# A two-layer hybrid transformer on one core: the projection gets weight memory of its own, and the attention's PSUM is split two ways for its high output and three for scores

## The chip, the cores and the metric

One core of one Trainium2 chip runs the whole program. The metric is device time in microseconds (us). TensorE multiplies, VectorE (DVE), ScalarE (ACT) and GpSimd (POOL) do the elementwise work, and SyncE (SP) issues most DMAs. "Half clock" below means TensorE's granted clock of 1.2 GHz instead of 2.4.

## The reference, cut to what matters

All arithmetic is float32, over 2048 tokens of width 1024 and a context prefix of 256 tokens.

```python
# layer 0: 8 latent heads (keys of 64+32) and 8 grouped-query heads (2 key heads of 64)
h = modulate(x, shift, scale) @ w_in                  # and the same for the context
o_a = softmax(q_a k_a^T * A_SCALE) v_a                # 2048 queries, 256 + 2048 keys, 16 heads
o_b = softmax(q_b k_b^T * B_SCALE) v_b
y = concat([o_a * silu(g_a), o_b * silu(g_b)]) @ w_out
x = layer_norm(ALPHA * x + gate * y)
# layer 1: gated MLP that mixes tokens in chunks of 128
u, v, g = split(modulate(x, shift, scale) @ w_in)
v = layer_norm(gelu(v)); mixed = w_s @ v + b_s
y = (gelu(u) * mixed * silu(g)) @ w_out
out = layer_norm(ALPHA * x + gate * y)
```

## The kernel before

Each float32 operand of a large product is split into a high part (rounded to TensorE's fp32r format) and a low part (the rest), and a product is the sum of two or three fp32r matmuls. `split` makes the two parts: on ScalarE and VectorE, or, with `pool`, both on GpSimd.

There are three phases. **phase1** (0 to about 690 us) projects the inputs and writes keys, queries, values and gates to DRAM. **attention** (about 690 to 2357 us) works through 64 items, one per head and block of 512 queries (`work`, head by head): items 0 to 31 are latent heads, 32 to 63 grouped-query heads. An item has 18 steps, one for each 128 keys. For a step, `score` makes three (latent) or two (grouped-query) matmuls into a PSUM tile `s`, ScalarE takes the exponential twice (`ph` rounded to high, then in place in `s`), and `low` subtracts on VectorE: `pl = s - ph`, which frees `s`. In one or two steps of an item GpSimd makes both parts instead, from a copy `pf`. `mul` multiplies the values with `ph` into PSUM tile `oh` and with `pl` into `ol`. `add` sums `ph` on GpSimd for the softmax's denominator, and `total` splits that sum (`sh`, `sl`) for two more matmuls in the last `mul` of the item. `take` copies `ol` to `ob` on ScalarE, `finish` adds `oh` to it on VectorE (two instructions), multiplies by the gate (`gt`) and stores it. For a later item, 18 `peak` matmuls into PSUM tile `m` and 18 maxima on VectorE (`mx`) find the largest score of each query row. The last of them gives `nm`, which goes to DRAM (`NM`) and comes back as a row of the queries (`q<-NM`, `row`). The first scores of that item need that row.

The eight PSUM banks are: four for `s`, two for `m`, one each for `oh` and `ol`. The order of the work is written out by hand: `at(time, unit)` gives each unit a time in steps, the units are sorted by it, and `InOrder` keeps the instructions of one engine in that order. In step s there are: `score` at s, `mul` at `place` + 0.3, `peak` at s + 0.6, the maximum 0.7 later, `low` at s + 1.6. `place` lies 4 steps behind the score, plus `LATE[t]` for the first steps of an item, since `oh` and `ol` must be read first. For the last four items (the same head) there are no `add`s, and the gate is multiplied on VectorE. While they run, `z_load` and `z_split` prepare the first 512 tokens of the projection's input on GpSimd. `recip` inverts the denominators by way of DRAM.

**phase3** (about 2357 us to the end) takes four blocks of 512 tokens: the projection by `e_w_out` (`token_major`, PSUM `acc`) with norm, transposes (`tp`), then the second layer. `weights` loads 512 KB and splits it. Its first calls are gathered in `pre`, split on GpSimd. Instructions not bound by `InOrder` are placed by the compiler where their operands and memory are ready. Memory is laid out in the order of the pools and of the first use of a tag, and a tile waits for whatever tile lay in its place. In phase3 the pool `p3`, which holds the weight tiles `w`, `wh`, `wl`, the residual `t` and `gate_e`, lies in place of the attention's tiles, and the pool `p3c` of constants above it, in memory that the attention doesn't use.

Of the kernel before, what the change touches and what calls it, by code (L numbers as in the profile page):

```python
# [19 lines left out]
P = 128  # L20
D = 1024
# [36 lines left out]
def split(e, h, l, src, pool=False):  # L58

    if pool:  # L60
        e.nc.gpsimd.tensor_scalar(out=h, in0=src, scalar1=1.0, scalar2=0.0, op0=ALU.mult, op1=ALU.add)
        e.nc.gpsimd.tensor_tensor(out=l, in0=src, in1=h.bitcast(F32), op=ALU.subtract)  # L62
    else:
        e.nc.scalar.activation(h, src, AF.Copy)  # L64
        e.nc.vector.tensor_tensor(out=l, in0=src, in1=h.bitcast(F32), op=ALU.subtract)  # L65
# [462 lines left out]
def z_split(e, hl, z, pool=False):  # L528
    nc = e.nc
    h, l = hl  # L530
    (nc.gpsimd if pool else nc.vector).tensor_tensor(out=z, in0=l.bitcast(F32), in1=h.bitcast(F32), op=ALU.mult)
    split(e, h, l, z, pool)
# [111 lines left out]
def attention(e):  # L644
# [6 lines left out]

    LATE = (3.0, 2.6, 2.2, 1.8, 1.4, 1.0, .6, .3)
    with tc.tile_pool(name="atc", bufs=1, reuse_waits="tile") as cp, \
# [36 lines left out]
        def score(s):  # L690
# [4 lines left out]
            ks = slice(t * P, (t + 1) * P)  # L695
            ps = pp.tile([P, CH], F32, name="s", tag="s", bufs=4)
            m = NOPE + ROPE
# [43 lines left out]
        def mul(s):  # L741
# [3 lines left out]
            if t == 0:  # L745
                gates[i] = sp.tile([P, CH], F32, name="gt", tag="gt", bufs=2)
                nc.sync.dma_start(gates[i][:DV], e.G[h * DV:(h + 1) * DV, g * CH:(g + 1) * CH])
                acc[i] = [pp.tile([P, CH], F32, name="o" + q, tag="o" + q, bufs=1) for q in "hl"]
            ph, pl, _ = pts.pop(s)
# [16 lines left out]
        def finish(i):  # L766
            h, g = work[i]
            cs = slice(g * CH, (g + 1) * CH)
            ob, (oh, ol) = outs.pop(i), acc.pop(i)
            DVE.tensor_tensor(out=ob[:DV], in0=oh[:DV], in1=ob[:DV], op=ALU.add)  # L770
            DVE.tensor_tensor(out=ob[:DV], in0=oh[DV:], in1=ob[:DV], op=ALU.add)
            (DVE if i >= NW - NG else POOL).tensor_tensor(out=ob[:DV], in0=ob[:DV], in1=gates.pop(i)[:DV], op=ALU.mult)
            nc.sync.dma_start(e.SU[h:h + 1, cs], ob[DV:DV + 1])
            (nc.scalar if i == NW - 1 else nc.sync).dma_start(e.O[h * DV:(h + 1) * DV, cs], ob[:DV])

        def recip(b):

            view = lambda t: t[:, b * CH:(b + 1) * CH].rearrange("h (p j) -> h p j", p=8)
            rs = sp.tile([P, CH // 8], F32, name="rs", tag="rs", bufs=2)
            nc.sync.dma_start(rs, view(e.SU))  # L780
            nc.vector.reciprocal(rs, rs)
            nc.sync.dma_start(view(e.R1), rs)

# [16 lines left out]
        for s in range(NW * NTT):  # L800
# [8 lines left out]
            place = s + (LAGP if t in parts else LAG + (LATE[t] if t < len(LATE) else 0))  # L809
            at(place + 0.3, mul, s)  # L810
            if t == NTT - 1:
# [17 lines left out]
        for k in range(NK):  # L829
            at(end - (NG - 1) * NTT + 4 * k + 17, lambda k: z_split(e, e.Z[0][k], sp.tile([P, CH], F32, name="zt", tag="zt", bufs=2), True), k)  # L830
        for _, _, (f, *args) in sorted(units):
# [3 lines left out]
def phase3(e):  # L835
    nc, tc, I = e.nc, e.tc, e.ins
    NB = SEQ // CH
    with tc.tile_pool(name="p3", bufs=2, reuse_waits="tile") as sp, \
            tc.tile_pool(name="p3c", bufs=1, reuse_waits="tile") as cp, \
            tc.tile_pool(name="p3ps", bufs=1, space=PSUM, reuse_waits="tile") as pp:  # L840
# [26 lines left out]
        def late_constants():  # L867
# [4 lines left out]
            C["wsl"] = cp.tile([P, 8, P], F32R, name="wsl")  # L872
            w = sp.tile([P, 8, P], F32, name="w", tag="w", bufs=2)
            nc.sync.dma_start(w, I["wsT"])
# [4 lines left out]
        def wtile(q):  # L879
            return sp.tile([P, 1024], F32R if q else F32, name="w" + q, tag="w" + q, bufs=3 if q else 2)  # L880

# [65 lines left out]
        def even_out(b, Z, X, T, halfway=None, stagger=False, pre=()):  # L947
# [14 lines left out]
            token_major(Z, I["e_w_out"], 0, evac, halfway, b == 0, pre)  # L962
            if b == 0:
                constants()
            for k in range(NK):
# [7 lines left out]
        def odd_in(b, X, Z, T, v):  # L973
# [28 lines left out]
            for j in range(16):  # L1002
# [20 lines left out]
                if b + 1 < NB:  # L1023
                    if 2 <= j < 10:
                        z_split(e, Z[j - 2], tmp("y", 3))
                    if j < len(Z.groups):
                        z_load(e, b + 1, Z.groups[j], nc.gpsimd)
                if 4 <= j < 8:
                    nc.gpsimd.tensor_tensor(out=T[:, j - 4, :], in0=T[:, j - 4, :], in1=C["eg"], op=ALU.mult)
                    nc.gpsimd.tensor_tensor(out=T[:, j - 4, :], in0=T[:, j - 4, :], in1=C["eb"], op=ALU.add)  # L1030
            gated(7, st)
# [6 lines left out]
        def odd_out(b, Z, T):  # L1038
            xr = [T[:, t, :] for t in range(4)]

            def evac(t, cc, ps):
# [9 lines left out]


        w, h = ([wtile(q) for i in range(2)] for q in ("", "h"))
        ge, T = (sp.tile(x, F32, name=n, bufs=1) for n, x in (("gate_e", [P, D]), ("t", [P, 4, D])))
        l = [wtile("l") for i in range(2)]
        pre = [weights(I["e_w_out"].rearrange("(k p) f -> p k f", p=P)[:, 2 * kk:2 * kk + 2, :CH], 2, (h[kk], l[kk]), w[kk], True)
               for kk in range(2)]
        C["gate_e"] = ge
        nc.sync.dma_start(ge, e.M[0].partition_broadcast(P))
        residual(0, T, nc.sync)  # L1060
        V = sp.tile([P, 4, D], F32, name="v", bufs=1)
        A, B = e.Z[0], ring(e, True)
# [131 lines left out]
```

## Time and profile before

| | |
|---|---|
| median of 3 runs | 3374.85 us (3371.83 to 3386.05) |
| profiled execution, time and span | 3379.72 us, 3377.9 us |
| TensorE busy | 3209.4 us, 95% of the span, 13,698 matmuls |
| VectorE, ScalarE, GpSimd busy | 2555.7, 1890.6, 1763.6 us |

The profile is of one execution. Busy time counts an engine's own instructions, and a TensorE that is busy all the time can still run at half clock. Times in rows are microseconds from the start of the span. Engines: PE is TensorE's matmuls, SPq the queue of SyncE.

### The profile page before, as it was taken

The page shows a single profiled execution, that of the slowest core. Times are in us where ns is not written, and L with a number is a line of the kernel's source. Part 1 is how long each engine was busy: PE and PEld are TensorE (multiplying, and loading weights), DVE is VectorE, ACT ScalarE, POOL GpSimd, SP SyncE. Part 2 cuts the span into 40 slices and gives each one's busy share as a digit, 9 for nine tenths or more (in the row PEclk, how much of TensorE's full clock was granted, in tenths as well). Part 3 has the DMA queues.
Part 4 walks back from the last instruction along what each step waited for, and adds up shares of the span by engine and source line. Part 5 has one row for each costly group of instructions (what it writes and reads, how often), then busy time and mean ns, then how long its engine had stood idle before and what let it go on. Part 6 is the DMA issues. An engine that isn't in the chain of part 4 may idle for free.

```text
span 3377.9 us, 40485 instructions
## 1 busy us (share of the span) xinstructions
PE 3209.4 (95%) x13698; PEld 2435.5 (72%) x13698; DVE 2555.7 (76%) x3626; ACT 1890.6 (56%) x3259; POOL 1763.6 (52%) x1413
## 2 busy tenths in 40 slices
PE   7999999989999999999999999997899999999998
PEld 3886777767777777776666666665678778778786
DVE  4847894688888888888988989897655765855846
ACT  3433342267777777777777777775243353353342
POOL 3312431279999999998888888842302301301201
PEclk9999999999999999999999999998899999999999
DMA  6456655642212322122101111112533433433332
GB/s 229 141 166 203 205 165 166 176 89 59 60 37 50 63 59 59 35 54 62 28 25 27 36 40 27 29 29 38 167 100 106 132 117 107 140 107 108 106 94 75
DMA packets 187185, 314.09 MB, mean 93 GB/s; under 512 B 53264, under 2 KB 79184, under 8 KB 185056
## 3 DMA queue, kind: packets, MB, share of 16 engines
q1 hardware_dynamic: 179088, 284.08, 30.0%
q0 software_dynamic: 7808, 27.28, 2.6%
q8 instruction: 108, 1.77, 0.3%
q14 instruction: 101, 0.83, 0.2%
q10 hardware_dynamic: 80, 0.13, 0.0%
HBM read 240.71 MB, written 70.73 MB: 92 GB/s over the span
## 4 chain that ended last, share of the span: by engine, by line
PE 68%; DVE 7%; DMA 5%; issue 4%; ACT 2%; POOL 1%; SPq 0%; POOLq 0%; ACTq 0%; DVEq 0%
PE s L587 17%; PE ol L587 10%; PE oh L587 7%; PE m L587 7%; PE acc L910 4%; PE acc L911 3%; PE acc L1008 3%; PE acc L1007 3%; PE acc L1009 3%; PE acc L912 3%; DMA NM<-nm 3%; DVE mx L587 2%; PE ps L175 1%; PE ps L176 1%; PE ps L177 1%
## 5 line engine op out<-in xcount | busy, mean ns | idle before, releaser
L587 POOL TENSOR_TENSOR sa<-sa,ph 128x512 f32<-128x512 f32 x728 | 939.1, 1290 | 70.7 <-ACT ph L587 24.9
L587 DVE TENSOR_REDUCE mx<-m 128x1 f32<-128x512 f32 x1124 | 768.7, 686 | 154.3 <-PE m L587 128.6
L587 PE MATMUL s<-q,k 96*128 96x512 f32 (+2 forms) x2880 | 867.9, 399 | 12.0 <-DMA q<-NM 11.5
L587 ACT ACTIVATE ph<-s 128x512 fp32r<-128x512 f32 x1064 | 634.1, 596 | 337.8 <-PE s L587 320.0
L587 DVE TENSOR_TENSOR pl<-s,ph 128x512 fp32r<-128x512 f32 x1064 | 726.0, 683 | 41.6 <-ACT s L587 39.8
L587 PEld LDWEIGHTS s<-q,k 96*128 96x128 f32 (+2 forms) x2880 | 543.2, 190 | 151.6 <-issue 10.6
L587 ACT ACTIVATE s<-s 128x512 f32<-128x512 f32 x1064 | 633.4, 595 | 0.0
L587 PE MATMUL m<-k,q 128*128 128x512 f32 (+1 forms) x1250 | 457.6, 383 | 34.2 <-DVE mx L587 30.9
L587 PE MATMUL oh<-ph,v 128*128 128x512 f32 x1152 | 461.1, 400 | 14.3 <-DVE ob L587 13.5
L587 PE MATMUL ol<-pl,v 128*65 128x512 f32 x1152 | 455.5, 395 | 0.0
L64 ACT ACTIVATE wh<-w 128x1024 fp32r<-128x1024 f32 x154 | 163.2, 1059 | 492.2 <-PE acc L912 233.1
L65 DVE TENSOR_TENSOR wl<-w,wh 128x1024 fp32r<-128x1024 f32 x154 | 220.0, 1429 | 276.5 <-ACT wh L64 276.2
L587 PEld LDWEIGHTS m<-k,q 128*128 128x128 f32 (+1 forms) x1250 | 228.8, 189 | 173.0 <-DVE mx L587 88.9
L1018 POOL TENSOR_TENSOR u<-u,y 128x512 f32<-128x512 f32 x32 | 63.5, 1984 | 417.7 <-ACT y L1017 417.7
L587 PEld LDWEIGHTS oh<-ph,v 128*128 128x128 f32 x1152 | 218.3, 190 | 85.0 <-PE s L587 24.2
L176 PE MATMUL ps<-xl,wh 128*128 128x512 f32 (+1 forms) x640 | 251.3, 393 | 7.5 <-DVE xl L167 7.5
L175 PE MATMUL ps<-xh,wh 128*128 128x512 f32 (+1 forms) x640 | 250.6, 392 | 6.6 <-POOL wh L146 4.0
L177 PE MATMUL ps<-xh,wl 128*128 128x512 f32 (+1 forms) x640 | 249.8, 390 | 1.6 <-DVE wl L147 1.6
L587 PEld LDWEIGHTS ol<-pl,v 128*65 128x65 f32 x1152 | 158.7, 138 | 49.1
L910 PE MATMUL acc<-wh,k 128*128 128x512 f32 x384 | 158.6, 414 | 34.4 <-DVE y L1044 18.8
L911 PE MATMUL acc<-wl,k 128*128 128x512 f32 x384 | 157.5, 410 | 1.2 <-POOL wl L62 1.2
L146 POOL TENSOR_SCALAR wh<-wr 128x1024 fp32r<-128x1024 f32 (+1 forms) x48 | 57.9, 1207 | 189.9 <-PE ps L176 119.3
(300 smaller groups left out, 5458.8 us busy)
## 6 DMA issues: line engine op xcount, KB each, us to landing
w<-in_wug SPq DMA_DIRECT2D x64, 512.0 KB
wr<-in_w SPq DMA_DIRECT2D x38, 512.0 KB
w<-in_e_w_out SPq DMA_DIRECT2D x32, 512.0 KB
w<-in_o_w_in SPq DMA_DIRECT2D x32, 512.0 KB
w<-in_o_w_out SPq DMA_DIRECT2D x32, 512.0 KB
wr<-in_e_w_mod SPq DMA_DIRECT2D x24, 512.0 KB
wr<-in_o_w_mod SPq DMA_DIRECT2D x24, 512.0 KB
q<-QB SPq DMA_DIRECT2D x96, 128.0 KB
```

Of the source, the lines that this page charges most:

```text
L64: e.nc.scalar.activation(h, src, AF.Copy)
L65: e.nc.vector.tensor_tensor(out=l, in0=src, in1=h.bitcast(F32), op=ALU.subtract)
L175: nc.tensor.matmul(out, lhsT=wh(k), rhs=xh(k), start=i == 0, stop=False)
L176: nc.tensor.matmul(out, lhsT=wh(k), rhs=xl(k), start=False, stop=False)
L177: nc.tensor.matmul(out, lhsT=wl(k), rhs=xh(k), start=False, stop=i == n - 1)
L587: i = getattr(self.engine, name)(*args, **kw)
L910: nc.tensor.matmul(ps[t], lhsT=h[:, ts], rhs=w[0][:, k, :], start=first, stop=False)
L911: nc.tensor.matmul(ps[t], lhsT=h[:, ts], rhs=w[1][:, k, :], start=False, stop=False)
L912: nc.tensor.matmul(ps[t], lhsT=l[:, ts], rhs=w[0][:, k, :], start=False, stop=last)
L1007: nc.tensor.matmul(ps, lhsT=w[0][:, k, :], rhs=h, start=k == 0, stop=False)
L1008: nc.tensor.matmul(ps, lhsT=w[0][:, k, :], rhs=l, start=False, stop=False)
L1009: nc.tensor.matmul(ps, lhsT=w[1][:, k, :], rhs=h, start=False, stop=k == NK - 1)
```

## The change

It has these parts. In the attention: `oh` gets two PSUM banks and `s` three. `LATE` is shortened to four smaller delays. `mul` is placed 0.4 of a step later, which puts it behind `peak` in each step. The gate is always multiplied on GpSimd, and `z_split` there joins the written order. For the last four items the output goes by GpSimd's queue, and for the last the other small DMAs by ScalarE's. In phase3: the pools are laid out in another order (constants lowest, then the working tiles, then a new pool `p3w` for weight tiles, `gate_e` and the residual), three weight tiles are made ahead instead of two, `constants()` is called before the projection, and the four tiles of the residual are scaled and shifted in eight calls spread over eight passes instead of four.

```diff
 def split(e, h, l, src, pool=False):
     if pool:
-        e.nc.gpsimd.tensor_scalar(out=h, in0=src, scalar1=1.0, scalar2=0.0, op0=ALU.mult, op1=ALU.add)
-        e.nc.gpsimd.tensor_tensor(out=l, in0=src, in1=h.bitcast(F32), op=ALU.subtract)
+        pool = e.nc.gpsimd if pool is True else pool
+        pool.tensor_scalar(out=h, in0=src, scalar1=1.0, scalar2=0.0, op0=ALU.mult, op1=ALU.add)
+        pool.tensor_tensor(out=l, in0=src, in1=h.bitcast(F32), op=ALU.subtract)
...
 def z_split(e, hl, z, pool=False):
-    (nc.gpsimd if pool else nc.vector).tensor_tensor(out=z, in0=l.bitcast(F32), in1=h.bitcast(F32), op=ALU.mult)
+    (pool or nc.vector).tensor_tensor(out=z, in0=l.bitcast(F32), in1=h.bitcast(F32), op=ALU.mult)
...
-    LATE = (3.0, 2.6, 2.2, 1.8, 1.4, 1.0, .6, .3)
+    LATE = (1.2, .9, .6, .3)
...
-            ps = pp.tile([P, CH], F32, name="s", tag="s", bufs=4)
+            ps = pp.tile([P, CH], F32, name="s", tag="s", bufs=3)
...
-                acc[i] = [pp.tile([P, CH], F32, name="o" + q, tag="o" + q, bufs=1) for q in "hl"]
+                acc[i] = [pp.tile([P, CH], F32, name="o" + q, tag="o" + q, bufs=1 + (q == "h")) for q in "hl"]
...
-            (DVE if i >= NW - NG else POOL).tensor_tensor(out=ob[:DV], in0=ob[:DV], in1=gates.pop(i)[:DV], op=ALU.mult)
-            nc.sync.dma_start(e.SU[h:h + 1, cs], ob[DV:DV + 1])
-            (nc.scalar if i == NW - 1 else nc.sync).dma_start(e.O[h * DV:(h + 1) * DV, cs], ob[:DV])
+            POOL.tensor_tensor(out=ob[:DV], in0=ob[:DV], in1=gates.pop(i)[:DV], op=ALU.mult)
+            q = nc.scalar if i == NW - 1 else nc.sync
+            q.dma_start(e.SU[h:h + 1, cs], ob[DV:DV + 1])
+            (nc.gpsimd if i >= NW - NG else q).dma_start(e.O[h * DV:(h + 1) * DV, cs], ob[:DV])
...
-            nc.sync.dma_start(rs, view(e.SU))
+            q = nc.scalar if b == NG - 1 else nc.sync
+            q.dma_start(rs, view(e.SU))
             nc.vector.reciprocal(rs, rs)
-            nc.sync.dma_start(view(e.R1), rs)
+            q.dma_start(view(e.R1), rs)
...
-            at(place + 0.3, mul, s)
+            at(place + 0.7, mul, s)
...
-            at(end - (NG - 1) * NTT + 4 * k + 17, lambda k: z_split(e, e.Z[0][k], sp.tile([P, CH], F32, name="zt", tag="zt", bufs=2), True), k)
+            at(end - (NG - 1) * NTT + 4 * k + 17, lambda k: z_split(e, e.Z[0][k], sp.tile([P, CH], F32, name="zt", tag="zt", bufs=2), POOL), k)
...
-    with tc.tile_pool(name="p3", bufs=2, reuse_waits="tile") as sp, \
-            tc.tile_pool(name="p3c", bufs=1, reuse_waits="tile") as cp, \
+    with tc.tile_pool(name="p3c", bufs=1, reuse_waits="tile") as cp, \
+            tc.tile_pool(name="p3", bufs=2, reuse_waits="tile") as sp, \
+            tc.tile_pool(name="p3w", bufs=2, reuse_waits="tile") as wp, \
...
-            w = sp.tile([P, 8, P], F32, name="w", tag="w", bufs=2)
+            w = wp.tile([P, 8, P], F32, name="w", tag="w", bufs=2)
...
-            return sp.tile([P, 1024], F32R if q else F32, name="w" + q, tag="w" + q, bufs=3 if q else 2)
+            return wp.tile([P, 1024], F32R if q else F32, name="w" + q, tag="w" + q, bufs=3 if q else 2)
...
-            if b == 0:
-                constants()
...
-                if 4 <= j < 8:
-                    nc.gpsimd.tensor_tensor(out=T[:, j - 4, :], in0=T[:, j - 4, :], in1=C["eg"], op=ALU.mult)
-                    nc.gpsimd.tensor_tensor(out=T[:, j - 4, :], in0=T[:, j - 4, :], in1=C["eb"], op=ALU.add)
+                if 4 <= j < 12:
+                    t = (j - 4) // 2
+                    nc.gpsimd.tensor_tensor(out=T[:, t, :], in0=T[:, t, :], in1=C["eb" if j % 2 else "eg"], op=ALU.add if j % 2 else ALU.mult)
...
-        w, h = ([wtile(q) for i in range(2)] for q in ("", "h"))
-        ge, T = (sp.tile(x, F32, name=n, bufs=1) for n, x in (("gate_e", [P, D]), ("t", [P, 4, D])))
-        l = [wtile("l") for i in range(2)]
-        pre = [weights(I["e_w_out"].rearrange("(k p) f -> p k f", p=P)[:, 2 * kk:2 * kk + 2, :CH], 2, (h[kk], l[kk]), w[kk], True)
-               for kk in range(2)]
+        pre = [weights(I["e_w_out"].rearrange("(k p) f -> p k f", p=P)[:, 2 * kk:2 * kk + 2, :CH], 2, pool=True)
+               for kk in range(3)]
+        ge, T = (wp.tile(x, F32, name=n, bufs=1) for n, x in (("gate_e", [P, D]), ("t", [P, 4, D])))
         C["gate_e"] = ge
         nc.sync.dma_start(ge, e.M[0].partition_broadcast(P))
         residual(0, T, nc.sync)
+        constants()
```

## Rows read from the trace of the kernel before

**Rows 1.** Four stretches: length, busy us per engine, granted clock, DMA share, GB/s.
```profile
690.00:1540.00 850.00, 849.10 (x3649) 639.79 (x3648) 752.32 (x1221) 637.80 (x1187) 776.55 (x624) 1.00 0.26 55
1540.00:2240.00 700.00, 668.26 (x2797) 472.32 (x2796) 627.27 (x1037) 537.76 (x1008) 571.76 (x478) 0.99 0.14 34
...
2357.00:2376.00 19.00, 7.22 (x18) 5.13 (x18) 2.61 (x4) 0.87 (x2) 6.78 (x4) 0.64 0.67 243
2436.00:2458.00 22.00, 12.27 (x46) 9.50 (x46) 22.00 (x9) 2.70 (x4) 16.27 (x8) 0.77 0.11 32
```

**Rows 2.** Timeline, early latent-head attention: TensorE, then VectorE.
```profile
1027.80 0.86 PE L587 MATMUL s<-q,k 97*128 97x512 f32 x3
...
1032.02 0.86 PE L587 MATMUL s<-q,k 97*128 97x512 f32 x3
...
1030.02 0.68 DVE L587 TENSOR_TENSOR pl<-s,ph 128x512 fp32r<-128x512 f32 x1
```

**Rows 3.** Timeline, between two grouped-query items, TensorE. In brackets: idle, releaser.
```profile
1919.04 0.40 PE L587 MATMUL m<-k,q 128*128 128x512 f32 x1
...
1922.12 0.47 PE L587 MATMUL oh<-ph,v 128*128 128x512 f32 x1 [0.43 <-DVE ob L587]
...
1923.35 0.50 PE L587 MATMUL m<-k,q 128*128 128x256 f32 x2 [0.54 <-DVE mx L587]
```

**Rows 4.** Timeline, same stretch, VectorE.
```profile
1918.77 0.69 DVE L587 TENSOR_REDUCE mx<-m 128x1 f32<-128x512 f32 x1 [1.16 <-PE m L587]
...
1919.97 0.68 DVE L587 TENSOR_REDUCE mx<-m 128x1 f32<-128x512 f32 x1
1920.57 1.40 DVE L587 TENSOR_TENSOR ob<-oh,ob 64x512 f32<-64x512 f32 x2
...
1925.72 0.17 DVE L587 TENSOR_REDUCE nm<-mx 128x4 fp32r<-128x20 f32 x1
```

**Rows 5.** Chain of waits, order of time: start, length, what.
```profile
1975.44 10.95 DMA NM<-nm
1986.41 1.38 DMA q<-NM
```

**Rows 6.** Timeline near the attention's end: VectorE, GpSimd, TensorE.
```profile
2300.42 14.37 DVE L587 TENSOR_TENSOR ob<-ob,gt 64x512 f32<-64x512 f32 x1
...
2312.99 1.25 POOL L62 TENSOR_TENSOR q<-zt,q 128x512 fp32r<-128x512 f32 x1
...
2316.17 0.80 PE L587 MATMUL m<-k,q 128*128 128x256 f32 x2 [14.70 <-DVE mx L587]
```

**Rows 7.** Timeline, attention to projection: SyncE's queue, GpSimd, TensorE.
```profile
2362.29 1.11 SPq L884 DMA_DIRECT2D w<-in_e_w_out  x2
...
2366.65 1.04 POOL L61 TENSOR_SCALAR wh<-w 128x1024 fp32r<-128x1024 f32 x1 [52.41 <-DMA w<-in_e_w_out]
2367.78 2.35 POOL L62 TENSOR_TENSOR wl<-w,wh 128x1024 fp32r<-128x1024 f32 x1
...
2367.75 1.22 PE L910 MATMUL acc<-wh,k 128*128 128x512 f32 x2 [10.57 <-POOL wh L61]
```

**Rows 8.** Timeline, attention's start: SyncE's queue, GpSimd, VectorE.
```profile
690.28 0.43 SPq L849 DMA_DIRECT2D mg<-in_rows  x1
...
696.20 1.05 POOL L857 TENSOR_SCALAR eg<-eg 128x1024 f32<-128x1024 f32 x1
...
705.97 1.10 DVE L862 TENSOR_TENSOR mg<-mg,s 128x8 f32<-128x8 f32 x1
```

**Rows 9.** Timeline, end of the first item: GpSimd, TensorE.
```profile
717.38 1.29 POOL L587 TENSOR_TENSOR sl<-sa,sh 128x512 fp32r<-128x512 f32 x1 [0.74 <-ACT sh L587]
...
719.18 0.39 PE L587 MATMUL ol<-sh,last 128*65 128x512 f32 x1
```

**Rows 10.** Timeline after the first projection: VectorE, GpSimd.
```profile
2433.47 19.89 DVE L65 TENSOR_TENSOR wl<-w,wh 128x1024 fp32r<-128x1024 f32 x1 [0.29 <-ACT wh L64]
...
2447.65 4.62 POOL L1030 TENSOR_TENSOR t<-t,eb 128x1024 f32<-128x1024 f32 x2
```

## The prediction

> **What bounds the kernel now.** I read the busy times by stretch first. While the latent heads run, TensorE is busy in 849.10 of 850 us at full clock with 3649 matmuls, so a matmul costs 0.233 us there and nothing but fewer matmuls would shorten that stretch [rows 1]. While the grouped-query heads run, it is busy in 668.26 of 700 us: 31.7 us are lost, and no other engine is full (VectorE 627 us) [rows 1]. So each of those items is lost in at a place, which the timeline shows. Between two items TensorE waits 0.43 us for VectorE to read `oh` and 0.54 us for a maximum [rows 3], while just before VectorE had stood idle for 1.16 us, because the five matmuls of the last `mul` were ahead of the next `peak` [rows 4]. VectorE is then late with everything up to `nm` [rows 4], and from `nm` a chain of two DMAs leads to the next item's scores: 10.95 and 1.38 us, 12.33 together, and where this pair stands in the chain of waits TensorE waits for it [rows 5]. The 28 items of the stretch take 25 us each.
>
> Then there are two large single holes. Near the attention's end VectorE's multiplication by the gate takes 14.37 us instead of under one. It ends just after GpSimd's last `z_split` instruction (2312.99 + 1.25), and TensorE stands for 14.70 us behind it [rows 6]. Between attention and projection TensorE idles for 10.57 us, waiting for GpSimd's split of a weight tile whose load was issued only at 2362.29 [rows 7]. In the 19 us of that boundary 18 matmuls ran, at 0.64 of the clock [rows 1]. A third hole follows: a weight split on VectorE takes 19.89 us under the scaling of the residual on GpSimd [rows 10].
>
> **The change part by part.**
>
> *Latent heads (32 items), 0 us.* TensorE is full, so more room gains nothing. The cost could come from three score buffers instead of four: a score may start when `low` of the score three before is done. A score starts at 1027.80, its `low` ends at 1030.02 + 0.68 = 1030.70, and the third score after it starts at 1032.02: 1.32 us to spare [rows 2]. Between items VectorE puts in two `ob` instructions, 1.40 us [rows 4], which would eat that. But `peak` now stands ahead of `mul`, so VectorE is no longer starved before it, and the step with the long `mul` gives it 5 x 0.233 us more. I take 0; the bad end is a rival below.
>
> *Grouped-query items 32 to 59, -14 us.* The second `oh` bank removes the 0.43 us wait, and earlier `mul`s spread TensorE's burst of scores and maxima. Yet the item's period follows from the loop nm, DMA, row, scores, nm, so what counts is when `nm` comes. With `peak` first, the maximum that starts at 1918.77 has its input five matmuls (1.16 us) earlier. The next maximum cannot use all of that: its `peak` still stands behind the long `mul`, starts at 1919.04 as before, and takes 0.40 us, so with some 0.04 us of signal it can be read at 1919.48 instead of 1919.97 [rows 3, 4]. From there to `nm` VectorE works without a gap either way. So `nm` and with it the period come 0.49 us earlier; 28 items give 13.7. Bounds: 0, if the three score buffers take it back; 31.7, if all idle time of the stretch goes [rows 1]. I stay near the first term, since the 12.33 us of the DMA pair are untouched.
>
> *The last four items, -18 us.* The gate's multiplication leaves VectorE, and with it the 14.70 us hole. The halves of a `peak` that follow the hole took 0.80 us together [rows 6] against 0.50 elsewhere [rows 3], so the clock had fallen; 15.0 with this pair alone, up to 2 more if the following matmuls get it back. On GpSimd the multiplication stands in the written order among the `z_split`s, where only DMAs wait for it. If that cover is gone, the next `ob` buffer is late, which nothing on TensorE needs for an item. The two short waits of an item boundary, 0.97 us [rows 3], go at three boundaries: 3.
>
> The Trainium skill, "SBUF — State Buffer", section "Who interferes with whom", says that a VectorE instruction with two SBUF inputs contends with a GpSimd instruction that reads SBUF, and that the one that holds the shared ports blocks the other for a whole instruction. The 14.37 us agree with it as far as the blocking goes [rows 6]; a block that lasts over a whole stream of GpSimd instructions is more than it says.
>
> *Attention to projection, -14.8 us.* The weight tiles get memory above the constants and working tiles. By the tile sizes in the code these two pools take about 84 KB per partition, the attention's tiles about 75 KB, so the weights no longer lie over live tiles. What such a tile does can be read from the constants, which had the free memory before: loaded at 690, scaled on GpSimd at 696.20, though they belong to phase3 [rows 8]. So the three weight tiles will be loaded and split at the start of the attention, and the projection starts right behind the last `ol`, with three of four row groups of weights at hand (3 x 24 matmuls, 16.8 us of cover for the next ones). The 19 us of rows 1 then hold 18 matmuls' 4.2 us: 14.8 saved. Bound below: the splits stay behind the attention's last GpSimd instruction, and one split (1.04 + 2.35 us [rows 7]) and the start remain, about 7 saved.
>
> *Start of the attention, +7 us.* GpSimd gets three splits, 3 x 3.39 = 10.2 us [rows 7], and loses two scalings of 1.05 us [rows 8]: 8.1 more. It is late there already: `sl` ends at 718.67, TensorE's row of matmuls that need `sh` and `sl` begins at 719.18 [rows 9], so 0.74 us to spare for `sl`, one matmul later, and one matmul more since `peak` goes first. 8.1 - 1.0 = 7.1, once. Bounds: 0, if the splits come before the first sums; 10.
>
> *Constants to the boundary, 0.* They now lie over the attention's tiles and are loaded when it ends. The columns (`mg` and three more) are first read after the projection's 192 matmuls, 45 us; that hides them. *The residual's scaling in eight passes, 0:* the same eight instructions; at present the last ends at 2452.27 [rows 10], while TensorE has 192 matmuls and four passes of 24, 67 us, to do before the first pass they are written in, so a later written place does not hold them back. Queues: the last SU and the last `recip` pass from SyncE to ScalarE, the outputs of four items to GpSimd. Behind the `recip` write, which waits for VectorE's reciprocal, ScalarE has the split of the fourth weight tile, and that has the 16.8 us of cover; behind GpSimd's outputs stand `z_split`s that are needed only in the projection.
>
> *Sum:* -13.7 - 15.0 - 3 - 14.8 + 7.1 = -39.4, against the profiled execution's 3379.72, which gives 3340.3. That execution lies 4.9 us above the median of the runs shown, so the median should be 3374.85 - 39.4 = 3335.
>
> **The rivals.**
>
> A. *The forecast,* 3335, chance 0.44.
>
> B. *The row loop is looser than I take it,* and the grouped-query stretch falls to its matmuls: 31.7 instead of 13.7 saved, 3317. For it: the 12.33 us are the longer of what the chain shows. Against: in many items TensorE waits right there. 0.16.
>
> C. *The spread scaling works:* VectorE's split waits for at most an instruction or two of GpSimd instead of 19.89 us [rows 10]. The 22 us of that stretch held 46 matmuls, 10.7 us at full clock [rows 1], so up to 11.3 more are saved: 3324. Against: what was said of the written place. 0.12.
>
> D. *The constants stand in the way of the projection's weights.* Seven rows of 512 KB and four columns come at the boundary. Columns issued from 690.28 on were used at 705.97 [rows 8], so up to 15.7 us of queue; with some slack of the tiles at hand, about 10 of it shows: 3345. 0.10. The Trainium skill, "DMA: Bandwidth & Descriptors", section "Rules for kernel authors", says that a strided last dimension becomes one descriptor per element, which speaks against moving these columns into a busy stretch; it has no price for 1024 of them, and by the trace the whole set took no more than the 15.7 us.
>
> E. *Slower: three score buffers bind.* If VectorE's 1.40 us of `ob` [rows 4] reach TensorE at each boundary, the 60 items pay 84 us and the 13.7 are gone: 3335 + 84 + 13.7 = 3433. It decides from where `low` ends more than 1.32 us later than in rows 2; without the 13.7 us the other parts save 25.7, so 0.43 us an item cancels them and 0.71 makes the kernel slower by 0.5%. 0.08.
>
> F. *It does less:* GpSimd's stream blocks another VectorE instruction, so the 15.0 and the 3 are not saved, and the splits come late, so the boundary gives 7 and the start costs nothing: 3374.85 - 13.7 - 7 = 3354. 0.10.
>
> **How the numbers follow.** Half a percent, 17 us, is about what a measurement here tells from no change. The predicted time is A's, 3335. The range reaches from 3304 (B and C together, 3306) to 3360 (F with a few us of E); it leaves out E and little else. Faster by over 0.5% means below 3358: A, B, C, D and a little over half of F, 0.88, less 0.02 for what I have not thought of: 0.86. Within: the rest of F and the weak part of E, 0.08. Slower: 0.06.
>
> **What would show it.** In the changed profile the `ob<-ob,gt` on VectorE is gone, and no hole of over 10 us stands before the projection. `w<-in_e_w_out` appears near 690, with three GpSimd splits, and the first item's `ol<-sh` is some 7 us later against its scores. In a grouped-query item the wait of `oh` on `ob` is gone, `nm` comes earlier after the long `mul`, and the period is half a microsecond shorter. The latent items keep their 849 busy us in 850: if that stretch grows by more than the 7 us, E is at work and the prediction is wrong. The 19.89 us split is still there, or C holds.

## The result and the profile after

The changed kernel takes 3339.53 us (median of 4 runs, 3336.28 to 3342.20), the kernel before on the same chip 3377.81 us; the ratio is 0.988, 95% interval 0.9865 to 0.9897. The forecast was 3335 against 3374.85, which is 0.988 too. The profiled execution took 3341.19 us.

To compare stages I use borders that every trace has, all of them starts of matmuls: the first score, the 18th and last `oh<-ph,v` of items 0, 31, 59 and 63, and the first `acc`. The last column runs to the end of the span. Lengths in us, each from one profile; the experiments' rows are used below.

| kernel | first item | latent, 31 items | grouped-query, 28 | last four | boundary | behind |
|---|---|---|---|---|---|---|
| before | 31.0 | 821.5 | 701.1 | 115.0 | 11.4 | 1010.2 |
| after | 40.7 | 814.4 | 685.9 | 95.4 | 0.7 | 1016.3 |
| order_only | 33.3 | 854.9 | 688.1 | 113.6 | 11.3 | 1007.0 |
| banks_only | 32.6 | 820.3 | 726.5 | 120.4 | 11.2 | 1009.0 |
| order_banks | 32.7 | 813.0 | 673.8 | 97.1 | 11.2 | 1010.1 |
| gate_pool | 32.1 | 820.4 | 697.3 | 98.1 | 11.2 | 1005.7 |
| weights_memory | 34.4 | 826.1 | 700.8 | 99.9 | 0.7 | 1013.8 |
| after_again | 40.3 | 816.6 | 686.5 | 95.3 | 0.7 | 1016.2 |
| weights_pad | 40.9 | 816.2 | 687.0 | 95.4 | 0.7 | 1009.8 |
| start_split_vector | 36.0 | 814.9 | 685.8 | 95.4 | 0.7 | 1017.0 |
| ahead_spread | 40.8 | 814.4 | 673.9 | 94.3 | 0.7 | 979.6 |
| late_pad | 40.7 | 849.9 | 669.9 | 95.0 | 0.7 | 1003.4 |
| attention_pad | 40.3 | 816.1 | 685.7 | 95.1 | 0.7 | 1016.1 |
| joined | 37.4 | 814.4 | 664.0 | 93.9 | 0.7 | 971.9 |

From before to after that is +9.7, -7.1, -15.2, -19.6, -10.7 and +6.1, with -1.7 ahead of the first score (which lies between 680.8 and 689.8 in these traces): -38.5. The stretches of after, cut at round times (length, busy us of each engine with its instructions, clock, DMA share, GB/s):

```profile
686.00:727.00 41.00, 32.76 (x126) 24.92 (x127) 26.27 (x42) 22.93 (x43) 34.67 (x26) 0.87 0.60 169
727.00:1541.00 814.00, 811.25 (x3530) 621.71 (x3529) 725.13 (x1177) 616.60 (x1147) 750.47 (x603) 1.00 0.24 52
1541.00:2227.00 686.00, 665.68 (x2801) 472.47 (x2801) 633.39 (x1039) 537.88 (x1009) 570.93 (x478) 1.00 0.14 34
2227.00:2323.00 96.00, 93.79 (x404) 66.88 (x403) 78.16 (x125) 76.16 (x142) 32.13 (x31) 1.00 0.24 41
2323.00:3339.00 1016.00, 965.89 (x4194) 773.47 (x4192) 630.25 (x741) 394.01 (x532) 194.04 (x132) 0.98 0.37 112
```

TensorE is now busy in 94 of 96 us of the last items, where the hole of [rows 6] was, but in the first item for only 33 of 41.

The latent items got shorter, though [rows 1] had shown TensorE busy in all but 0.9 of 850 us. This is the opening of an item before, on TensorE's timeline (start, length, instruction; x3 is three in a row):

```profile
989.58 0.86 PE L587 MATMUL s<-q,k 97*128 97x512 f32 x3
990.34 0.47 PE L587 MATMUL oh<-ph,v 128*128 128x512 f32 x1
990.65 0.39 PE L587 MATMUL ol<-pl,v 128*65 128x512 f32 x1
990.98 0.50 PE L587 MATMUL m<-k,q 96*128 96x256 f32 x2
991.31 0.40 PE L587 MATMUL oh<-ph,v 128*128 128x512 f32 x1
```

and the same place after:

```profile
993.30 0.40 PE L588 MATMUL oh<-ph,v 128*128 128x512 f32 x1
993.54 0.40 PE L588 MATMUL ol<-pl,v 128*65 128x512 f32 x1
993.78 0.85 PE L588 MATMUL s<-q,k 97*128 97x512 f32 x3
994.46 0.40 PE L588 MATMUL m<-k,q 96*128 96x256 f32 x2
994.70 0.39 PE L588 MATMUL oh<-ph,v 128*128 128x512 f32 x1
```

Look at the starts. After, from `oh` to `ol` to the next it is 0.24 us each. Before, `oh` starts 0.31 us ahead of `ol`, that one 0.33 ahead of the maximum, and `oh` itself 0.06 late behind the third score (989.58 + 3 x 0.234 = 990.28). A matmul counts as busy for 0.39 us while the next may start after 0.23; so a wait of up to 0.16 us leaves no idle time in the view. The two half maxima held the next `oh` for 0.33 us (990.98 to 991.31), after for 0.24 (994.46 to 994.70). Together, 0.06 + 0.07 + 0.09 + 0.09, these are 0.31 of the 0.37 us that an ordinary latent item lost (medians 26.48 and 26.11). In the first items of six heads the change costs 0.2 to 0.3 us instead, so the 31 items gained 7.1 us and not 11.5.

A grouped-query item after: TensorE, then VectorE.

```profile
1816.43 0.40 PE L588 MATMUL ol<-pl,v 128*65 128x512 f32 x1
1817.31 0.74 PE L588 MATMUL s<-q,k 128*128 128x512 f32 x2 [0.49 <-DVE pl L588]
...
1815.13 1.40 DVE L588 TENSOR_TENSOR ob<-oh,ob 64x512 f32<-64x512 f32 x2
...
1820.28 0.17 DVE L588 TENSOR_REDUCE nm<-mx 128x4 fp32r<-128x20 f32 x1
```

The wait of [rows 3] for `ob` is gone, as forecast. In its place a score waits 0.49 us for `pl`: the two `ob` instructions, 1.40 us, stand ahead of it, and there are three score buffers. From 1545 to 2220 us, by the waits of TensorE (total us, times, longest):

```profile
PE s L588 <- DVE pl L588: 13.8, 28, 0.5
PE s L588 <- DMA q<-NM: 5.7, 12, 2.3
```

The second line is the row; it ends a wait in 12 places here. Waits too short for this view show in the starts again: of the two matmuls of an item's first score only the second needs the row, and it starts 0.23 us behind the first when the row is there. What these pairs take beyond that adds up to 10.1 us in the 28 items, 3.4 in the kernel before.

Start and end of the hoisted weights: SyncE's queue and GpSimd at the attention's start, TensorE at its end.

```profile
687.39 1.05 SPq L888 DMA_DIRECT2D w<-in_e_w_out  x2
...
694.42 1.05 POOL L62 TENSOR_SCALAR wh<-w 128x1024 fp32r<-128x1024 f32 x1
...
697.04 4.76 POOL L63 TENSOR_TENSOR wl<-w,wh 128x1024 fp32r<-128x1024 f32 x2
...
723.11 1.26 POOL L588 TENSOR_TENSOR sl<-sa,sh 128x512 fp32r<-128x512 f32 x1 [0.74 <-ACT sh L588]
...
2322.86 0.40 PE L588 MATMUL ol<-pl,v 128*65 128x512 f32 x1
2323.10 0.40 PE L914 MATMUL acc<-wh,k 128*128 128x512 f32 x1
```

[rows 7] have become a projection that starts 0.24 us behind the last `ol`. `sl` comes at 723.11 instead of 717.38 [rows 9]; against the first score that is 37.1 us behind it instead of 29.7. Last, the residual's passes on GpSimd, VectorE's weight split and TensorE behind the first projection:

```profile
2385.94 5.51 POOL L1032 TENSOR_TENSOR t<-t,eg 128x1024 f32<-128x1024 f32 x2
...
2405.88 3.36 DVE L66 TENSOR_TENSOR wl<-w,wh 128x1024 fp32r<-128x1024 f32 x1
...
2409.29 0.79 PE L915 MATMUL acc<-wl,k 128*128 128x512 f32 x1 [8.36 <-DVE wl L66]
2409.88 0.63 PE L916 MATMUL acc<-wh,k 128*128 128x512 f32 x1
2410.31 0.63 PE L914 MATMUL acc<-wh,k 128*128 128x512 f32 x1
```

The eight passes still run back to back, from 2385.94 to 2408.15. The split is 3.36 us instead of 19.89 [rows 10], but it stands behind other VectorE instructions that got in at one per GpSimd instruction, and TensorE waits 8.36 us; behind the wait it starts a matmul every 0.43 us. The granted clock is 1.2 GHz (0.50) from 2404.8, within the wait, to 2415.0:

```profile
2404.80:2415.00 10.20, 5.71 (x13) 4.31 (x14) 8.56 (x8) 4.50 (x7) 3.35 (x2) 0.50 0.22 57
```

### The profile page after: what moved, and what is told of

Its sections match the earlier page's. It is cut to its first block, busy times and chain, and to the rows that moved or that the text cites. A ratio compares the mean times of both kernels' runs of the same rounds, so it can differ in the third digit from the quotient of the medians.

```text
span 3339.4 us, 40476 instructions
## 1 busy us (share of the span) xinstructions
PE 3200.2 (96%) x13698; PEld 2435.2 (73%) x13698; DVE 2541.0 (76%) x3621; ACT 1890.9 (57%) x3258; POOL 1777.9 (53%) x1423
## 4 chain that ended last, share of the span: by engine, by line
PE 52%; DMA 10%; POOL 8%; DVE 8%; issue 5%; ACT 3%; SPq 0%; POOLq 0%; ACTq 0%; DVEq 0%
PE s L588 12%; POOL sa L588 6%; PE ol L588 6%; DMA NM<-nm 6%; PE oh L588 4%; PE m L588 4%; PE acc L1011 4%; PE acc L1010 4%; PE acc L1009 4%; PE acc L915 3%; PE acc L914 3%; PE acc L916 3%; DVE pl L588 2%; DMA q<-NM 2%; DMA w<-in_o_w_in 1%
## 5 line engine op out<-in xcount | busy, mean ns | idle before, releaser
L588 PE MATMUL s<-q,k 96*128 96x512 f32 (+2 forms) x2880 | 874.3, 400 | 40.8 <-DVE pl L588 22.9
L66 DVE TENSOR_TENSOR wl<-w,wh 128x1024 fp32r<-128x1024 f32 x153 | 202.2, 1321 | 267.6 <-ACT wh L65 266.8
L914 PE MATMUL acc<-wh,k 128*128 128x512 f32 x384 | 159.7, 416 | 24.1 <-DVE y L1046 18.6
L916 PE MATMUL acc<-wh,k 128*128 128x512 f32 x384 | 156.9, 409 | 0.0
```

Of the source, the lines that this page charges most:

```text
L588: i = getattr(self.engine, name)(*args, **kw)
L914: nc.tensor.matmul(ps[t], lhsT=h[:, ts], rhs=w[0][:, k, :], start=first, stop=False)
L916: nc.tensor.matmul(ps[t], lhsT=l[:, ts], rhs=w[0][:, k, :], start=False, stop=last)
```

## The experiments

Ratios are to the kernel before, run on the same chip; the kernels of each of the three groups shared a chip, but for `joined`, which ran on another.

**Order and banks of the attention, apart and together; the gate alone.** `order_only` and `order_banks` change

```
-    LATE = (3.0, 2.6, 2.2, 1.8, 1.4, 1.0, .6, .3)
+    LATE = (1.2, .9, .6, .3)
...
-            at(place + 0.3, mul, s)
+            at(place + 0.7, mul, s)
```

in the kernel before, `banks_only` and `order_banks`

```
-            ps = pp.tile([P, CH], F32, name="s", tag="s", bufs=4)
+            ps = pp.tile([P, CH], F32, name="s", tag="s", bufs=3)
...
-   ... name="o" + q, tag="o" + q, bufs=1) ...
+   ... name="o" + q, tag="o" + q, bufs=1 + (q == "h")) ...
```

and `gate_pool` the line of the gate, with `POOL` as the engine of `z_split` and `split` as in the change:

```
-            (DVE if i >= NW - NG else POOL).tensor_tensor(out=ob[:DV], ...
+            POOL.tensor_tensor(out=ob[:DV], ...
```

> The kernel before with only the written order of the attention changed: four late starts of up to 1.2 steps instead of eight of up to 3.0, and each mul 0.4 of a step later, behind the peak of its step. One bank for the high output and four for scores stay. Theory 1 (order and second bank hang together): the first mul of an item now comes 1.4 steps sooner, some 1.9 us, while VectorE still reads the single high output; TensorE waits for it about 1 us in each of 60 items, the latent stretch grows from 821.5 us by 20 to 40, the grouped-query stretch stays near 701, and the time is 3395 to 3430. Theory 2 (the order by itself brings nm half a microsecond forward): grouped-query stretch 687 us, latent 821, time about 3362.

3397.61 us, ratio 1.009 (1.006 to 1.0121): theory 1, with 33 us lost in the latent stretch to one wait (waits of TensorE there):

```profile
PE oh L587 <- DVE ob L587: 37.9, 30, 1.3
```

But in the grouped-query items the order gained 13 us all the same, with as long a wait for `ob` in each.

> The kernel before with only the PSUM banks changed: two for the high output, three for scores, the written order as before. Theory 1 (the 7.1 us that the latent stretch gained come from the high output's bank, because the oh that opens an item no longer waits for VectorE): latent stretch 814 us instead of 821.5, grouped-query stretch 690 to 695 instead of 701 (the 0.43 us wait of 28 items), time 3360 to 3366. Theory 2 (the gain comes from the order, and three score buffers cost by themselves): latent stretch 821 or more, grouped-query stretch over 701, time 3376 to 3400.

3405.25 us, 1.0123 (1.009 to 1.0155): theory 1 fails, and theory 2's upper end of 3400 is passed. Rival E's wait is there, in the grouped-query items, at its full 1.5 us:

```profile
PE s L587 <- DVE pl L587: 41.5, 27, 1.5
```

In the latent items `oh` no longer waits, and the next maximum does (0.47 us from start to start):

```profile
987.24 0.40 PE L587 MATMUL ol<-pl,v 128*65 128x512 f32 x1
987.71 0.50 PE L587 MATMUL m<-k,q 96*128 96x256 f32 x2
```

so these gained only 1.2 us. VectorE's two `ob` instructions delay whatever it does next; which bank that shows in is a matter of the order.

> The kernel before with order and banks of the attention changed, and nothing else (gate, weight memory and residual as before). Theory 1 (the attention's gain is whole in these two): latent stretch 814, grouped-query stretch 686, the three boundaries of the last four items 2 to 3 us less; the 14.70 us hole and the 10.57 us boundary stay; 7 + 15 + 3 = 25 us, time about 3351. Theory 2 (the gate on GpSimd has a part in it, since VectorE lost instructions in the last items): latent and grouped-query stretches as said, but less than 2 us in the last four.

3320.96 us, 0.9874 (0.9837 to 0.9911): as much as the whole change, and 30 us under theory 1. Order and banks, each a loss by itself, gain together. The stages show two things that neither theory had. The grouped-query stretch is 12 us shorter than in after (below), and the last four items have lost their hole, though the gate is still on VectorE there (VectorE, then GpSimd):

```profile
2256.22 0.82 DVE L587 TENSOR_TENSOR ob<-ob,gt 64x512 f32<-64x512 f32 x1
...
2255.30 1.20 POOL L61 TENSOR_SCALAR k<-zt 128x512 fp32r<-128x512 f32 x2
2256.47 2.94 POOL L62 TENSOR_TENSOR k<-zt,k 128x512 fp32r<-128x512 f32 x2
```

> The kernel before with only the gate multiplications of the last four items moved from VectorE to GpSimd, in the written order among the z_splits. Theory 1 (the hole is VectorE's multiplication starved under GpSimd's stream): the stretch of the last four items falls from 115.0 to about 100 us, no ob<-ob,gt on VectorE, time 15 us less, about 3361. Theory 2 (what starves is whatever two-input instruction VectorE has next under that stream): another VectorE instruction, pl or ob, takes over 10 us at the same place, the stretch stays over 110 us, time 3373 to 3378.

3351.19 us, 0.9951 (0.9935 to 0.9967): theory 1, 16.9 us off the last four items. So either edit removes the hole, and the two can't be added. What goes with it is the same in all five traces with the gate on VectorE. Where it starts while GpSimd is in an instruction with two inputs, it ends with GpSimd's stream: 14.37 us before [rows 6], 14.61 in order_only, 12.10 in banks_only. Where it starts within a `TENSOR_SCALAR`, one input, it takes 0.82 us (order_banks, above) and 0.68 (weights_memory). In these two it started in the last 0.28 and 0.13 us of the pair of `TENSOR_SCALAR`s, and GpSimd's next pair took 2.94 and 2.96 us where the pair ahead had taken 2.55 and 2.53: there it seems to be GpSimd that waited. These are five cases, and no run varied the start by itself. If any start within the `TENSOR_SCALAR`s will do, the windows are 1.2 us wide and come about every 6 us, so a shift of a microsecond can make or undo 15 us.

**The rest of the change, on one chip.** `after_again` is the changed kernel itself; `weights_memory` is the kernel before with the change's pools, `pre` and place of `constants()`, and the old line of the residual.

> The changed kernel once more, beside the three others of this group on one chip. Theory 1 (the time of a grouped-query item hangs on how soon its row lands, which differed by some 0.3 us between the profiles so far): where the row lands in time the period is 24.0 us as with order and banks alone, and the kernel takes 3325 to 3334; then all else that the change does brings nothing beside order and banks. Theory 2 (something else of the change, gate, queues or weights, slows the grouped-query items): period 24.3 to 24.4 again, 3336 to 3342.

3339.06 us, 0.9889 (0.9871 to 0.9908): theory 2's numbers. Whether the kernel or the chip makes the difference to order_banks can be read from the row's first DMA, in all traces. From the end of `nm` to the issue of the row's load, which waits for that DMA, it is 8.40 to 8.44 us (median of 28 items) in all four kernels of the first group, with the old order and the new, and 8.71 to 8.87 in the ten other traces. So it is the chip: the row lands 0.3 us sooner there.

> The kernel before with only the projection's part of the change: weight tiles with memory of their own, three of them split on GpSimd ahead, constants at the boundary. Theory 1 (the boundary gains 10.7, the start of the attention loses 8, and matmuls that read the moved weight tiles start 0.234 instead of 0.228 us apart, some 6 us in all): stages before the boundary unchanged but for the first item's 8 us, boundary under 1 us, projection and after 1015 us, total within 6 us of the kernel before. Theory 2 (as forecast: 14.8 gained, 7.1 lost, nothing else): 8 us faster.

3368.34 us, 0.9979 (0.9965 to 0.9994). The boundary fell by 10.7 us and the start lost 8 (first item and latent stretch together), near what both theories say; the stretch behind the attention grew by 3.6. By the profile the last four items lost their hole too, which by the paragraph above is luck of the shift; without those 15 us the part costs what it gains. The total alone would fit theory 2 (8 us faster); by its stages it is theory 1, with half of the growth behind.

In the changed kernel, `weights_pad` adds the first of these lines ahead of `pre`, `start_split_vector` changes the second:

```
+        wp.tile([P, 8], F32, name="pad", bufs=1)
-        pre = [weights(..., 2, pool=True)
+        pre = [weights(..., 2)
```

> The changed kernel with 32 bytes per partition left free ahead of the weight tiles, nothing else. Theory 1 (the pace of the projection's matmuls depends on where the moving weight tile begins in SBUF; in the kernel before it began at 96 modulo 128 bytes, in the changed one at 64, here at 96 again): acc<-wh,k starts fall from 0.234 to 0.227 to 0.230 us apart, the stretch behind the attention from 1016 to 1006 to 1011 us. Theory 2 (the pace differs between executions, or comes from contention with other engines): 0.234 us and 1016 us as in the changed kernel.

3336.50 us, 0.9878 (0.9863 to 0.9892); the stretch behind is 6.5 us shorter. The same matmuls, `acc<-wh,k` and its partners with four short transposes among them, in 40 us without a wait: before, after, with the pad (the number in brackets behind PE's busy time is what started):

```profile
2591.70:2631.70 40.00, 40.00 (x179) 32.82 (x178) 22.46 (x34) 9.22 (x11) 0.00 (x0) 1.00 0.33 101
```

```profile
2543.20:2583.20 40.00, 40.00 (x173) 32.16 (x172) 21.66 (x33) 9.19 (x10) 0.00 (x0) 1.00 0.32 100
```

```profile
2546.20:2586.20 40.00, 40.00 (x174) 32.16 (x174) 21.78 (x33) 9.18 (x10) 0.00 (x0) 1.00 0.30 101
```

These three paces, 0.2257, 0.2311 and 0.2302 us from start to start over 180 starts, repeat to 0.0001 us in every kernel that has the weight tiles at that place (gate_pool 0.2257, weights_memory 0.2312). So the place sets the pace, but not by its remainder modulo 128 bytes, which the pad had restored. Nor is it all: without the transposes the paces are 0.228, 0.234 and 0.233, and in the next block of the same kernels 0.230, 0.232 and 0.233.

> The changed kernel with the three weight splits at the start of the attention on ScalarE and VectorE (1.06 and 1.3 us each) instead of GpSimd. Theory 1 (the 9.8 us that the first item grew are GpSimd's 10.2 us of splits ahead of its sums): from the first score to the first item's last mul 33 to 36 us instead of 40.8, some 4 to 7 us less in all, about 0.15%. Theory 2 (VectorE is the scarcer engine, and its three subtractions delay maxima and low parts as much): 38 to 42 us, no gain.

3336.82 us, 0.9875 (0.9856 to 0.9893): the first item is 36.0 us instead of 40.3 to 40.7, theory 1. In the total the 4 us don't stand out from the interval.

**Row, residual, additions, places.** `ahead_spread`:

```
-AHEAD = 10
+AHEAD = 11
...
+            POOL = InOrder(tc, nc.gpsimd)
...
-                    nc.gpsimd.tensor_tensor(out=U[j - 8], in0=U[j - 8], in1=y, op=ALU.mult)
+                    POOL.tensor_tensor(out=U[j - 8], in0=U[j - 8], in1=y, op=ALU.mult)
+                    t = (j - 8) // 2
+                    POOL.tensor_tensor(out=T[:, t, :], in0=T[:, t, :], in1=C["eb" if j % 2 else "eg"], ...)
...
-                if 4 <= j < 12:
-                    (its two lines)
```

> The changed kernel with two edits in stages that don't touch: in the attention the maxima and the row of an item run 11 steps ahead of its scores instead of 10, and behind it the eight passes of the residual on GpSimd are bound in order, one behind each product with u, so that they can't run back to back. Attention, theory 1 (the row sets the grouped-query period, 24.4 us, and with a step more it lands in time): the wait for q<-NM goes, the period falls to the 24.0 us at which the three score buffers hold it, stretch 686 to 672-675 us. Theory 2 (nm comes later by what the row is asked for earlier, since one loop holds both): 684 to 688. Residual, theory 1 (rival C, and the waits of 3.6 and 3.2 us in each later block are VectorE's weight splits under the same eight instructions): no TensorE wait over 2 us there, stretch behind the attention 1016 to 992-1005 us. Theory 2 (each pass merely stalls VectorE where it now stands): 1012 to 1020. Time 3302 to 3325 if both first theories hold.

3291.40 us, 0.9747 (0.9731 to 0.9763). Both first theories, the second with more than was expected: behind the attention 979.6 us instead of 992 to 1005, and so the total lies 11 us under its range. The grouped-query period is 23.95 to 24.03 us in 26 of 28 items; the row's wait is gone and the score buffers' is left:

```profile
PE s L588 <- DVE pl L588: 13.3, 28, 0.5
PE s L588 <- DMA q<-NM: 1.6, 2, 1.2
```

So the row had set after's period. Where it lands in time, here and on the chip of order_banks, the score buffers hold the item at 24.0. Behind the attention TensorE's waits for VectorE and ScalarE, after and then here:

```profile
PE acc L914 <- DVE y L1046: 18.6, 6, 3.9
PE acc L915 <- DVE wl L66: 9.1, 2, 8.4
PE acc L914 <- ACT v L978: 3.1, 1, 3.1
PE acc L914 <- ACT t L978: 2.4, 1, 2.4
```

```profile
PE tp L999 <- DVE u L1000: 9.3, 4, 2.3
PE acc L914 <- ACT t L978: 0.8, 1, 0.8
```

That is 33.2 us against 10.1; the other 13.6 of the 36.7 gained I put down to the half clock around the waits. The granted clock fits: behind the attention TensorE was at 1.2 GHz for 50.6 us in after and for 17.5 here, and 33 us less at half clock are worth up to 16.5.

`late_pad` splits `finish` in two, one addition each, and moves them for items before the last four; its pad is 424 elements:

```
-                at(place + 2.3, finish, i)
+                for part in range(2):
+                    at(place + (2.3 if i >= NW - NG else 5.5 + 1.1 * part), finish, i, part)
```

> The changed kernel with two edits in stages that don't touch: the two additions that read the high output (all but the last four items) stand 3.2 and 4.3 steps later on VectorE, one each behind the item's nm, and the weight tiles begin 1696 bytes higher, at 1248 modulo 2048 bytes as in the kernel before. Attention, theory 1 (the wait of some 0.65 us at each item is three score buffers under 1.4 us of additions on VectorE): that wait on pl goes and nm comes a microsecond sooner, so the row wait goes too; period 23.5 to 23.8, grouped-query stretch 658 to 668 instead of 686. Theory 2 (VectorE is nearly full, and the additions delay as much where they now stand): 680 to 690. Weights, theory 1 (the place within 2048 bytes sets the pace): acc<-wh,k 0.227 to 0.229 us as before, stretch behind the attention 1005 to 1010. Theory 2 (which other tiles are read meanwhile counts too): some other pace between 0.229 and 0.235.

3346.48 us, 0.9910 (0.9896 to 0.9925). Grouped-query items: 23.63 us in most, no wait on `pl` any more; a short one for the maxima is left:

```profile
PE m L588 <- DVE mx L588: 5.2, 27, 0.2
```

The stretch misses theory 1's 668 by 2 us, since its first item is 30.1. But the latent stretch lost 35.5 us, which I had not expected: 0.3 in each item and 2 to 7 in each first item of a head. In SyncE's queue the line that issues `SU` now waits up to 13.5 us (after: 7.3) for `ob`:

```profile
SPq L775 <- ACT ob L588: 226.1, 31, 13.5
```

Keys and rows stand behind it there; that this is the cause is argued, not shown. The weights' pace is that of before to 0.0001 us (0.2258), and the stretch behind 12.9 us shorter, 1003.4 (theory 1: 1005 to 1010):

```profile
2563.00:2603.00 40.00, 40.00 (x179) 32.83 (x178) 22.50 (x34) 9.25 (x11) 0.00 (x0) 1.00 0.32 102
```

So the place modulo 2048 bytes decides, or something that goes with it.

`attention_pad` leaves 32 bytes free ahead of the attention's tiles:

> The changed kernel with 32 bytes per partition left free ahead of the attention's working tiles, nothing else. Theory 1 (as in the projection, the place of a moving tile sets the pace of the matmuls that stream it): oh and ol, 0.233 us from start to start, change by 0.002 to 0.005 us either way, and the latent stretch by 3 to 9 us. Theory 2 (the attention's pace is at its floor wherever the tiles lie): no change over 1 us in any stretch, 3336 to 3342.

3336.27 us, 0.9884 (0.9861 to 0.9906). Theory 2: `ol` starts move by 0.001 us, no stretch by more than 2.

`joined` takes AHEAD, residual, pad of 424 elements and the start's splits on ScalarE and VectorE, and the late additions for the 28 grouped-query items only.

> The changed kernel with all edits that gained in their stage: the three weight splits at the start on ScalarE and VectorE; maxima and row 11 steps ahead; in the grouped-query items alone the two additions that read the high output behind the item's nm; the weight tiles 1696 bytes higher; the residual's passes bound one behind each product with u. Theory 1 (each works in its own stage, so the stage gains add up): first item 36 us, latent stretch 814, grouped-query stretch 661 to 666, last four 94, boundary 0.7, stretch behind the attention 965 to 970; time 3258 to 3268. Theory 2 (the late additions cost in the grouped-query items once the row is early, or block SyncE's queue as they did in the latent stretch, 850 instead of 814 us): grouped-query stretch 674 or more, 3270 to 3290.

3272.69 us (3268.75 to 3274.80), 0.9686 (0.9663 to 0.9708): faster than both kernels, 5 us over theory 1's range. The grouped-query items are nearly down to their matmuls (23.7 us each; 100 starts of 0.233 are 23.3), and the stretch behind stays 2 us above its range:

```profile
1536.50:2200.50 664.00, 661.96 (x2802) 462.62 (x2801) 621.80 (x1038) 531.66 (x1010) 572.54 (x477) 1.00 0.16 35
2295.00:3267.00 972.00, 942.26 (x4193) 765.05 (x4192) 592.78 (x741) 393.99 (x532) 191.26 (x132) 0.99 0.39 117
```

## Why the prediction was right, and where its terms were not

The total came out within 1 us of the sum for the profiled execution (3341.19, 3340.3), partly by luck: two wrong terms, -7.1 and +6.1, cancelled, and a third came near for reasons that only half hold.

*Latent heads, 0: wrong, -7.1.* The step that failed is "TensorE is full, so more room gains nothing". It was read from the busy share, which hides waits under 0.16 us. Three score buffers cost nothing there (banks_only 820.3), so that half of the term held.

*Grouped-query items, -13.7: -15.2.* The size is right, and the loop that was named holds the changed kernel: a step more for the row brings 12 us more (ahead_spread). The prediction has it hold the kernel before as well, and there it held little: the DMA pair of [rows 5] stands in the chain of waits for 7 of the 28 items (15 after), and the row cost 3.4 us in all (10.1 after); what filled the old item were the two waits of [rows 3]. On the chip where the row lands in time the old order takes 24.70 us an item (gate_pool) and the new 23.98 (order_banks), 0.72 less. The row adds 0.14 to the old (24.84) and 0.40 to the new (24.38), which leaves 0.46. So the forecast 0.49 is the difference of a larger gain and a loss, and its closeness is partly luck. Rival B is false as a forecast, since the row does bind, but its 31.7 are there to be had (joined: 37.1 off 701.1). Rival E's mechanism exists in full; banks_only pays it, and the order is what keeps it to 0.5 us. That the order hides it was argued in the prediction for the latent items only.

*Last four items, -18: -19.6.* The hole goes, as gate_pool shows. But it was not a fixed property of the kernel before: order and banks alone shift the gate into a gap. So the gate's edit is worth 15 us only as insurance. The Trainium skill, "SBUF — State Buffer", section "Who interferes with whom", has a VectorE instruction with two SBUF inputs contend with GpSimd instructions that read SBUF. The runs agree that the two get in each other's way, and go beyond it: beside two-input instructions the gate was held not for one but for a whole stream (14.37 us).

*Attention to projection, -14.8: right.* The boundary lost 10.7, and the first 64 matmuls of the projection, whose first 7.5 us had been granted 1.2 GHz before, took 15.0 us instead of 19.1.

*Start, +7.1: +8.1.* That is 40.75 against the 32.65 of order_banks, whose later last `oh` is in both; it equals GpSimd's 8.1 us without the microsecond of slack that I took off. Moving the splits off GpSimd brings 4.7 of it back (start_split_vector).

*Behind, 0: +6.1.* The term that was missing: matmuls that stream the moved weight tiles start 2.4% later from one another, 10.2 us with the 4.1 above. late_pad took 12.9 off. Constants at the boundary cost nothing: no wait over a microsecond in the first 45 us of the projection, so rival D is out.

*Residual:* rival C's condition failed as forecast, the written place moved nothing; its price was far too low. Bound apart the passes are worth 36.7 us: the same eight instructions had held up VectorE's splits and evacuations in all four blocks, not in the first alone.

## What to carry to other kernels

Read the starts of matmuls, not their busy share, before a stretch is called full. When two edits each give the other its room, as an order and a bank do, run them apart and together: here 1.009 and 1.012 make 0.987. And where a long stream of one engine's instructions starves another engine, break the stream up before moving the victim.

## What was not expected of the hardware

- The pace of the matmuls that stream the weight tiles goes with where these lie in SBUF: 0.2257, 0.2302 or 0.2311 us from start to start for the same work, equal to 0.0001 us between kernels and chips. The weight tiles began at 1248, 1632 and 1600 modulo 2048 bytes. Why is open; in the attention a shift of 32 bytes moved nothing by more than 0.001 us.
- A VectorE multiplication took 0.68 to 0.82 us, or 12.1 to 14.6, and in all five traces the short ones began late in a one-input GpSimd instruction, the long ones in a two-input one of the same stream. That this decides is not shown by a run of its own.
- With the same attention code for those items, the grouped-query stretch took 673.8 us on one chip and 686 on two others. The first of the row's two DMAs lands 0.3 us sooner on the first chip, in every kernel run there; the old order shows less of it (697.3 and 700.8).
